# One level of Strassen's algorithm in the first MLP product of a two-layer hybrid backbone

## The chip, the core and the metric

The kernel runs on one core of one Trainium2 chip. The metric is the device time of one execution in microseconds. Five engines work beside each other, each in its own fixed order of instructions: PE multiplies matrices (PEld loads its weights), DVE is the vector engine, ACT the scalar engine, POOL the general one, SP issues transfers; POOL and ACT can issue them too.

## What is computed

Two layers over 512 latent tokens of 1024 features, and in the first layer 256 context tokens as well. Each layer has a mixer (recurrence, attention, pooling, one output projection) and an MLP, both behind a modulated norm and both added with a gate:

```python
def _mlp(h, w1, w2):
    return jnp.square(jax.nn.relu(h @ w1)) @ w2
...
        x = x + g1 * y_lat
        x = x + g2 * _mlp(_modulate(_rmsnorm(x, g_norm2[l]), sh2, sc2), w_ff1[l], w_ff2[l])
        if not last:
            h = h + cg1 * y_ctx
            h = h + cg2 * _mlp(_modulate(_rmsnorm(h, g_norm2[l]), csh2, csc2), w_ff1[l], w_ff2[l])
```

`w1` is 1024 x 4096, `w2` 4096 x 1024, all in fp32.

## The kernel before

All activations stand with features on the 128 partitions and tokens along the row. A product is done in three passes of float32r matmuls: every operand is split into a high part (an ACT cast) and a low part (what the cast left over, a DVE subtraction), and `mm3` (L241) adds high x high, high x low and low x high. Weights come in blocks of 128x1024 (512 KB), streamed in the order of use by `Weights` (loads three blocks ahead, four buffers `raw`; the split into `whi`, L142, and `wlo`, L143, two blocks ahead, ten buffers).

The end of the mixer takes the eight tiles of the output projection one after the other: PE's products `wo` go into one of two large accumulators (`psA`), DVE adds the gated result to the residual tile (`add_to`, L1189), ACT and DVE make the modulated tile's parts `xh` and `xl` (`scaled`, L467 and L468), and `square` adds the tile's squares to the running sum on POOL (`acc`, L456). The shift of the modulation is carried as two further columns, so that 770 columns stream in layer 0 and 514 in layer 1. The norm's 1/rms is not needed until the products come out: `nsum` (L478) and `spread` (L498) put it on all partitions as `rb`.

`ffn` works by chunks of 128 hidden features. For one chunk `gemm_mod` streams eight tiles x three passes x two column segments, 48 matmuls. `ff1_out` scales by `rb` (`tf`, L539), adds the bias and clips (ACT, L544, L546), squares, and keeps the high and low parts `hh` and `hl` in SBUF (L1255 to L1257). Eight chunks of the first product alternate with eight tiles of the second (`ff2`, 24 matmuls of a segment each), which adds its gated result to the resident residual tile (L1276). In layer 0's MLP, "fills" run on DVE between the chunks: 56 items of modulation for later (`mod_rows`, `junk`, L413), each of two passes over 128x1024.

The order on each engine comes from a scheduler in the building framework that follows the order of the code and the buffers' release; the mixer's steps are listed by hand in `ORDER`. SBUF holds 47 row buffers of 776 columns in two classes: 18 "flow" tiles whose names are in `FLOW`, and 29 others.

## Time and profile before

| | |
|---|---|
| three runs | 1651.52, 1651.87, 1656.19 us; median 1651.87 |
| profiled execution | span 1650.7 us (its only time), 24064 instructions |
| PE | 1582.8 us busy, 96% |
| PE weight load | 1380.6 us, 84% |
| DVE | 1122.0 us, 68% |
| ACT | 680.4 us, 41% |
| POOL | 368.2 us, 22% |
| mean granted PE clock | 0.978 of full speed |
| memory traffic | 184.57 MB, 112 GB/s |

The profile records one execution. Its page gives each engine's busy time, groups of like instructions with the idle time before them and what ended it, and the transfers. The trace behind it can be asked for timelines, windows and single tiles. A busy time counts instructions that overlap once.

The layers follow each other: layer 0's mixer until 443 us, its MLP until 985, layer 1's mixer until 1283, its MLP until the end.

### The profile page before, as it was taken

The numbers are of one execution on the slowest core, as the hardware profiler recorded it, in microseconds if no ns is written. First come the engines' busy times: TensorE is split into PE (matmuls) and PEld (weight loads), VectorE is DVE, ScalarE is ACT, GpSimd is POOL, SyncE is SP. The second block draws the span as 40 slices with busy tenths as digits, with TensorE's granted clock in tenths as the row PEclk, the third lists the DMA queues.
The fourth block names the chain that finished last, engine by engine and source line by source line (L and its number), as shares of the span: only waits on it lengthen the run. The fifth ranks groups of instructions, "written<-read, shape, count | busy, mean of one in ns | idle before, by whom it ended". The sixth has DMA issues, their size and how long they took to land.

```text
span 1650.7 us, 24064 instructions
## 1 busy us (share of the span) xinstructions
PE 1582.8 (96%) x9519; PEld 1380.6 (84%) x9519; DVE 1122.0 (68%) x1810; ACT 680.4 (41%) x1078; POOL 368.2 (22%) x376
## 2 busy tenths in 40 slices
PE   5989999999999999999999999888999999999998
PEld 3668888889888888888888889787888989989897
DVE  8797888998767557837737646698987654545352
ACT  5557556646433123123213333745665432323131
POOL 4175434542300000000000232356454000000000
PEclk7999989999999999999999999999999999999999
DMA  6545211354234423524523430320334323323302
GB/s 251 198 150 185 81 58 37 94 185 152 82 97 144 142 89 119 187 78 128 166 90 120 142 109 21 121 71 20 97 122 141 103 90 96 97 90 93 100 27 102
DMA packets 54016, 184.57 MB, mean 112 GB/s; under 512 B 6624, under 2 KB 7264, under 8 KB 53904
## 3 DMA queue, kind: packets, MB, share of 16 engines
q1 hardware_dynamic: 49680, 166.49, 31.0%
q0 software_dynamic: 4224, 16.55, 2.8%
...
## 4 chain that ended last, share of the span: by engine, by line
PE 76%; DVE 15%; issue 4%; ACT 3%; POOL 1%; DMA 1%; SPq 0%; DVEq 0%; ACTq 0%; POOLq 0%
PE f L241 55%; PE wo L241 5%; PE inps L241 4%; PE sc L241 3%; DVE wlo L143 3%; PE tp L914 2%; DVE p L897 1%; PE modps L369 1%; DVE junk L413 1%; PE qp L241 1%; PE pv L936 1%; PE pv L937 1%; DVE ptl L922 1%; PE gps L241 1%; PE kns L823 1%
## 5 line engine op out<-in xcount | busy, mean ns | idle before, releaser
L142 ACT CAST whi<-raw 128x1024 fp32r<-128x1024 f32 x210 | 219.6, 1048 | 657.2 <-PE f L241 550.7
L143 DVE TENSOR_TENSOR wlo<-raw,whi 128x1024 fp32r<-128x1024 f32 x210 | 276.3, 1318 | 35.3 <-ACT whi L142 32.6
L241 PE MATMUL f<-xh,whi 128*128 128x258 f32 (+2 forms) x1024 | 234.6, 310 | 1.0 <-DVE tf L539 1.0
L241 PE MATMUL f<-xl,whi 128*128 128x258 f32 (+2 forms) x1024 | 234.5, 310 | 0.0
L241 PE MATMUL f<-xh,wlo 128*128 128x258 f32 (+2 forms) x1024 | 234.1, 310 | 0.0
L241 PE MATMUL f<-hh,wlo 128*128 128x512 f32 (+1 forms) x768 | 232.2, 356 | 0.0
L241 PE MATMUL f<-hl,whi 128*128 128x512 f32 (+1 forms) x768 | 231.9, 356 | 0.0
L241 PE MATMUL f<-hh,whi 128*128 128x512 f32 (+1 forms) x768 | 231.3, 356 | 0.0
L1276 DVE SCALAR_TENSOR_TENSOR xo<-f,mod,xo 128x512 f32<-128x512 f32 x96 | 60.5, 658 | 195.6 <-PE f L241 195.6
L413 DVE SCALAR_TENSOR_TENSOR junk<-modraw,cb 128x1024 bf16<-128x1024 f32 x128 | 161.8, 1275 | 21.9 <-DMA modraw<-in_wb_dram 21.5
L241 PEld LDWEIGHTS f<-xh,whi 128*128 128x128 f32 x1024 | 157.8, 189 | 12.5 <-PE f L241 1.2
L241 PEld LDWEIGHTS f<-xl,whi 128*128 128x128 f32 x1024 | 158.2, 189 | 11.4
L241 PEld LDWEIGHTS f<-xh,wlo 128*128 128x128 f32 x1024 | 157.9, 189 | 11.3
L539 DVE TENSOR_TENSOR tf<-f,rb 128x770 f32<-128x770 f32 (+1 forms) x64 | 52.8, 826 | 159.1 <-PE f L241 150.2
L241 PEld LDWEIGHTS f<-hh,whi 128*128 128x128 f32 x768 | 126.5, 188 | 22.4
L241 PEld LDWEIGHTS f<-hh,wlo 128*128 128x128 f32 x768 | 126.3, 188 | 22.5
L241 PEld LDWEIGHTS f<-hl,whi 128*128 128x128 f32 x768 | 126.4, 188 | 22.3
L463 POOL CAST xh<-mod 128x2 fp32r<-128x2 f32 x24 | 10.6, 441 | 466.8 <-PE f L241 466.8
L225 POOL TENSOR_SCALAR p<-p,sm 128x768 f32<-128x768 f32 (+1 forms) x80 | 70.4, 880 | 117.3 <-DVE sm L899 81.1
L241 PE MATMUL inps<-xh,whi 128*128 128x512 f32 (+1 forms) x352 | 87.3, 331 | 7.3 <-ACT xh L467 5.6
L305 ACT ACTIVATE p<-p,sm 128x768 f32<-128x768 f32 (+1 forms) x80 | 68.2, 853 | 57.4 <-DVE p L897 56.8
L241 PE MATMUL inps<-xl,whi 128*128 128x512 f32 (+1 forms) x352 | 86.4, 326 | 3.1 <-DVE xl L468 3.1
...
## 6 DMA issues: line engine op xcount, KB each, us to landing
...
kb<-kd POOLq DMA_DIRECT2D x16, 384.0 KB, 4.3
x<-in_x_dram SPq DMA_DIRECT2D x8, 384.0 KB, 7.0
xo<-in_x_dram SPq DMA_DIRECT2D x8, 384.0 KB, 3.4
xp<-xo POOLq DMA_DIRECT2D x8, 384.0 KB, 3.5
xo<-xp SPq DMA_DIRECT2D x8, 384.0 KB, 3.1
xd<-xo POOLq DMA_DIRECT2D x8, 256.0 KB, 2.4
```

Source lines behind the costliest of these rows:

```text
L142: nc.scalar.copy(hi, raw)
L143: nc.vector.tensor_tensor(lo, raw, hi.bitcast(F32), ALU.subtract)
L225: return self.nc.gpsimd.tensor_scalar(out, in_, scale, 0.0, ALU.mult, ALU.add)
L241: nc.tensor.matmul(ps, lhsT=a[:, ca], rhs=b[:, cb], start=first and i == 0, stop=last and i == 2)
L305: ins = self.nc.scalar.activation(out, in_, func, **kw)
L369: nc.tensor.matmul(ps[0:4, :], lhsT=self.ct[:, kk * 2 + j, :], rhs=w[:, j * 512:(j + 1) * 512], start=(kk == 0 and j == 0 and i == 0), sto ...
L413: nc.vector.scalar_tensor_tensor(junk, r, 1.0, c, ALU.mult, ALU.mult, accum_out=acc[l, g][:, v * 16 + i:v * 16 + i + 1])
L539: nc.vector.tensor_tensor(t[:, 0:n], ps[:, o:o + n], self.rb[:, 0:n], ALU.mult)
L823: nc.tensor.matmul(ps[:, tt:tt + 7:6], lhsT=sq[:, tt * 128:(tt + 1) * 128], rhs=self.cst[:, CST_SELK:CST_SELK + 2], start=True, stop=True)
L897: nc.vector.tensor_scalar(p[:, 0:keys], s, rq[:, qt:qt + 1], None, ALU.mult, ALU.min, accum_out=nb)
L914: nc.tensor.transpose(ps[:, j * 256 + q * 128:j * 256 + (q + 1) * 128], ps2[q][:, kt * 128:(kt + 1) * 128], self.ident)
L1276: nc.vector.scalar_tensor_tensor(x[:, a:a + e], ps[:, a:a + e], mod[:, v, 8 + m:9 + m], x[:, a:a + e], ALU.mult, ALU.add)
```

## The change

The 1024 x 4096 product is cut into 2 x 2 x 2 blocks: features in two halves of four tiles (`KORD` pairs tile j with j + 4), hidden features in two halves (chunk u with u + 16), tokens in two halves of 384 (layer 0) or 256 columns, each with two shift columns, 386 or 258. One level of Strassen's algorithm in Winograd's form makes seven products of them. A "unit" is a pair of chunks: seven products of four tiles x three passes, 84 matmuls; 16 units a layer. Products 1, 2, 6, 5 and 7 run in the unit, 3 and 4 after the first product of the next one.

For the stream, `stream_ops` makes per pair of tiles four differences on POOL and seven split operands `xq` (ACT cast, DVE subtraction), kept for the whole first product. For the weights, `weight_ops` makes per unit three differences on DVE (`ws`: t7, t6, t3); the sum of two blocks is made by a DMA that POOL issues and that adds one half of a loaded block to a half of the other, in SBUF. Seven split operands `wo` of 128x512 follow. From the accumulators, ACT copies three products out, DVE adds three and scales by `rb`.

All of the first product runs before all of the second. The hidden values go to memory unsplit (`hd`, issued by ACT) and the residual tiles too (`xf`, issued by POOL); the second product loads its hidden tiles again, one per tile of output, and splits them. Of the fills, 20 run in the first product and 36 in the second; those of layer 1 that nobody reads for the context are left out (`streams`).

The core of the diff:

```diff
-    "a2 acc gate hh hl inv knsq latn lsq mix p ps2 pth ptl pvt qlh qll rb t th u yh ylru z",
-    "a2 gate hh hl latn lsq lxp mxl p ps2 pth ptl pvt qlh qll row sq t th u yl ylru z",
+    "a2 acc gate inv knsq latn lsq mix p ps2 pth ptl pvt qlh qll rb t th u yh ylru z xz ya yb rr hz xr tt",
+    "a2 gate latn lsq lxp mxl p ps2 pth ptl pvt qlh qll row sq t th u yl ylru z xz ya yb rr hz xr tt",
 )
 NSLOT, NFLOW = 29, 18
-NGF = D_FF // 128 // GF
+NCH = D_FF // 128
+UNITS = NCH // 2
+GF = 8
+NGROUP = NCH // GF
+GROUPS = tuple(tuple(u + h * UNITS for u in range(g * GF // 2, (g + 1) * GF // 2) for h in range(2)) for g in range(NGROUP))
+KORD = tuple(j + h * KD // 2 for j in range(KD // 2) for h in range(2))
+FIRST, LATER = (1, 2, 6, 5, 7), (3, 4)
...
-        while self.split < min(len(self.order), at + 1 + self.splits):
+        while self.split < min(self.loaded, at + 1 + self.splits):
             name = self.order[self.split]
+            if name[1] == "ff1":
+                self.split += 1
+                continue
...
+    def get_raw(self, name):
...
+        self.loads = 1 if self.order[min(self.at + 4, len(self.order) - 1)][1] == "ff1" else 3
+        self.advance(self.at)
+        self.at += 1
+        return self.raw.pop(name)
...
+        def add_to(h, i, src):
+            acc, _ = pss.pop((h, i))
+            m = KORD[i]
             x = self.slot("xo")
...
-        s, sh = self.norm_scale(l, 2)
-        self.X, self.xs2 = [None] * KD, [None] * KD
-        for m in range(KD):
-            if m == 0:
+        ff = self.ff = FeedForward(self, l)
+        for i in range(KD):
+            if i == 0:
                 for j in [j for h, j in pss]:
                     project(1, j, LATE[-1:])
-            elif (1, m) not in pss:
-                project(1, m, LATE)
-            self.X[m] = add_to(1, m, self.xp[l])
-            self.xs2[m] = self.scaled(m, self.X[m], s, sh, ctx)
-            self.square(m, self.X[m], n)
...
+            elif (1, i) not in pss:
+                project(1, i, LATE)
+            ff.stream(i, add_to(1, i, self.xp[l]))
...
+class FeedForward:
+    def __init__(self, K, l):
+        self.K, self.nc, self.l = K, K.nc, l
...
+        self.n = T if self.ctx else L
+        self.nh = self.n // 2
+        self.n1 = self.nh + 2
+        self.s, self.sh = K.norm_scale(l, 2)
+        self.xq = [None] * (KD // 2)
...
+        self.jobs = [Hidden(self, u) for u in range(UNITS)]
+    def parts(self, hi, lo, src):
+        self.nc.scalar.copy(hi, src)
+        self.nc.vector.tensor_tensor(lo, src, hi.bitcast(F32), ALU.subtract)
+    def stream_ops(self, blocks, n, q):
+        nc, sub = self.nc, ALU.subtract
+        b11, b12, b21, b22 = blocks
+        def part(p, src):
+            q[p] = self.K.slot("xq", F32R)
+            self.parts(q[p][:, 0:n], q[p][:, n:2 * n], src)
...
+        part(1, b11)
+        part(2, b21)
+        nc.gpsimd.tensor_tensor(t[5], b12, b11, sub)
+        nc.gpsimd.tensor_tensor(t[6], b22, t[5], sub)
+        part(6, t[6])
+        part(5, t[5])
+        nc.gpsimd.tensor_tensor(t[7], b22, b12, sub)
+        nc.gpsimd.tensor_tensor(t[4], b21, t[6], sub)
+        part(7, t[7])
+        part(3, b22)
+        part(4, t[4])
+    def weight_ops(self, names, w):
+        nc, K = self.nc, self.K
+        a, t = [], {}
+        def part(p, src):
+            w[p] = K.wp.tile([128, 1024], F32R, tag="w", name="wo")
+            self.parts(w[p][:, 0:512], w[p][:, 512:1024], src)
+        def begin():
...
+            nc.vector.tensor_tensor(t[7], a[0], a[2], ALU.subtract)
+            nc.gpsimd.dma_start(out=a[2], in_=a[3], accum_op=ALU.add)
+            part(1, a[0])
+        def second():
+            nc.vector.tensor_tensor(t[6], a[2], a[0], ALU.subtract)
+            part(6, t[6])
+        def third():
+            nc.vector.tensor_tensor(t[3], a[1], t[6], ALU.subtract)
+            part(7, t[7])
+        return [begin, lambda: part(2, a[1]), second, lambda: part(5, a[2]), third, lambda: part(3, t[3]),
+                lambda: part(4, a[3])]
+    def product(self, ps, p, w, n, start):
+        for k in range(KD // 2):
+            wh, wl = (w[p][:, h * 512 + k * 128:h * 512 + (k + 1) * 128] for h in range(2))
+            xh, xl = self.xq[k][p][:, 0:n], self.xq[k][p][:, n:2 * n]
+            for j, (a, b) in enumerate(((wh, xh), (wh, xl), (wl, xh))):
+                self.nc.tensor.matmul(ps, lhsT=a, rhs=b, start=start and k == 0 and j == 0,
+                                      stop=k == KD // 2 - 1 and j == 2, skip_group_check=True)
+    def stream(self, i, x):
+        K, nc = self.K, self.nc
+        m = KORD[i]
...
+        nc.gpsimd.dma_start(out=K.xf[self.l, m, :, 0:self.n], in_=x[:, 0:self.n])
+        z = self.z[m] = K.slot("xz")
+        for c, e, v, t in self.pieces(2):
+            nc.scalar.activation(z[:, c:c + e], x[:, t:t + e], AF.Copy, scale=self.s[:, v, m:m + 1])
+        gap = z[:, 0:2 * self.n1].rearrange("p (h c) -> p h c", h=2)[:, :, self.nh:self.n1]
+        sh = self.sh[:, :, m].unsqueeze(1) if self.ctx else self.sh[:, 0, m:m + 1].unsqueeze(1)
+        nc.gpsimd.tensor_copy(gap, sh.to_broadcast([128, 2, 2]))
+        K.square(m, x, self.n)
+        if i % 2:
+            j = i // 2
+            n1 = self.n1
+            z1, z2 = self.z.pop(j), self.z.pop(j + KD // 2)
+            q = self.xq[j] = {}
+            self.stream_ops((z1[:, 0:n1], z1[:, n1:2 * n1], z2[:, 0:n1], z2[:, n1:2 * n1]), n1, q)
...
+    def load_hidden(self, c):
+        K, n = self.K, self.n
+        z = K.slot("hz")
+        K.load(z[:, 0:n], K.hd[self.l, c, :, 0:n])
+        hi, lo = K.slot("hh", F32R), K.slot("hl", F32R)
+        self.parts(hi[:, 0:n], lo[:, 0:n], z[:, 0:n])
+        self.h[c] = hi, lo
...
+    def run(self):
...
+        prev = None
+        for i, job in enumerate(self.jobs + [None]):
+            nxt = list(self.jobs[i + 1].prep) if i + 1 < len(self.jobs) else (
+                [lambda c=c: self.load_hidden(c) for c in GROUPS[0]] if job else [])
+            seq = [(job, p) for p in FIRST] if job else []
+            late = [(prev, p) for p in LATER] if prev else []
+            seq = seq[:1] + late + seq[1:]
+            for at, (jb, p) in enumerate(seq):
+                jb.do(p)
...
+                upto = -(-len(nxt) // (len(seq) - at))
+                for step in nxt[:upto]:
+                    step()
+                del nxt[:upto]
+            if job:
+                fill(early * (i + 1) // UNITS)
+            prev = job
+        self.x = {}
+        for m in KORD:
+            self.x[m] = K.slot("xr")
+            K.load(self.x[m][:, 0:self.n], K.xf[self.l, m, :, 0:self.n])
...
+class Hidden:
+    def __init__(self, ff, u):
+        self.ff, self.u, self.w = ff, u, {}
+        self.prep = ff.weight_ops([(ff.l, "ff1", c) for c in (u, u + UNITS)], self.w)
+    def do(self, p):
+        ff, K, nc = self.ff, self.ff.K, self.ff.nc
+        n = ff.n1
+        if p == 1:
+            self.bank = K.psA("f1")
+            self.ya, self.yb = K.slot("ya"), K.slot("yb")
+        b1, b3 = self.bank[:, 0:n], self.bank[:, 512:512 + n]
+        if p == 2:
+            self.other = K.psB("f1")
+        ps = {2: self.other[:, 0:n] if p == 2 else None, 5: b3, 3: b3}.get(p, b1)
+        ff.product(ps, p, self.w, n, p in (1, 2, 5))
+        half = slice(0, n), slice(n, 2 * n)
+        if p == 1:
+            nc.scalar.copy(self.ya[:, half[0]], ps)
+        elif p == 6:
+            nc.scalar.copy(self.ya[:, half[1]], ps)
+        elif p == 5:
+            nc.scalar.copy(self.yb[:, half[1]], ps)
+        elif p == 2:
+            nc.vector.tensor_tensor(self.ya[:, half[0]], ps, self.ya[:, half[0]], ALU.add)
+        elif p == 7:
+            nc.vector.tensor_tensor(self.yb[:, half[1]], ps, self.yb[:, half[1]], ALU.add)
+        elif p == 3:
+            nc.vector.tensor_tensor(self.ya[:, half[1]], ps, self.ya[:, half[1]], ALU.add)
+            nc.vector.tensor_tensor(self.ya[:, 0:2 * n], self.ya[:, 0:2 * n], ff.rb[:, 0:2 * n], ALU.mult)
+            self.out(self.u, self.ya)
+        else:
+            nc.vector.tensor_tensor(self.yb[:, half[0]], ps, ff.rb[:, half[0]], ALU.mult)
+            nc.vector.tensor_tensor(self.yb[:, half[1]], self.yb[:, half[1]], ff.rb[:, half[1]], ALU.mult)
+            self.out(self.u + UNITS, self.yb)
+    def out(self, c, y):
+        ff, K, nc = self.ff, self.ff.K, self.ff.nc
+        r = K.slot("rr")
+        for at, e, v, t in ff.pieces(2):
+            nc.scalar.activation(r[:, t:t + e], y[:, at:at + e], AF.Relu, bias=y[:, ff.nh + v:ff.nh + v + 1])
+        nc.scalar.activation(r[:, 0:ff.n], r[:, 0:ff.n], AF.Square)
+        nc.scalar.dma_start(out=K.hd[ff.l, c, :, 0:ff.n], in_=r[:, 0:ff.n])
...
-    rawp = ctx.enter_context(tc.tile_pool(name="raw", bufs=4))
+    rawp = ctx.enter_context(tc.tile_pool(name="raw", bufs=5))
     wp = ctx.enter_context(tc.tile_pool(name="wts", bufs=10))
...
-    nc = _bacc.Bacc("TRN2", target_bir_lowering=False, num_devices=1)
+    nc = _bacc.Bacc("TRN2", target_bir_lowering=False, num_devices=1, dynamic_dma_scratch_size=4096)
```

The order in which DVE's instructions stand at the end of layer 0's mixer, before, about the tiles in the middle (`xo<-wo` is the gated add, `xl` a low part, `wlo` that of weights):

```order
L1189 SCALAR_TENSOR_TENSOR xo<-wo,mod_1_975,xo 128x512
L1189 SCALAR_TENSOR_TENSOR xo<-wo,mod_1_975,xo 128x256
L468 SCALAR_TENSOR_TENSOR xl<-xo,s_2_4563,xh 128x512
L468 SCALAR_TENSOR_TENSOR xl<-xo,s_2_4563,xh 128x256
L143 TENSOR_TENSOR wlo<-raw,whi 128x1024
L1189 SCALAR_TENSOR_TENSOR xo<-wo,mod_1_975,xo 128x512
```

The same place on DVE after the change, from behind the adds of the second pair of tiles to the first add of the third (`ws` are the weight differences, `wo<-ws` and `wo<-raw` low parts of weights, `xq` those of the stream, `tt` POOL's differences):

```order
L1348 TENSOR_TENSOR ws<-raw 128x512
L1302 TENSOR_TENSOR xq<-xz,xq 128x386 x2
L1353 TENSOR_TENSOR ws<-raw 128x512
L1357 TENSOR_TENSOR ws<-raw,ws 128x512
L1302 TENSOR_TENSOR wo<-ws,wo 128x512
L1302 TENSOR_TENSOR wo<-raw,wo 128x512
L1302 TENSOR_TENSOR xq<-tt,xq 128x386 x2
L1302 TENSOR_TENSOR wo<-ws,wo 128x512 x2
L1302 TENSOR_TENSOR xq<-tt,xq 128x386
L1302 TENSOR_TENSOR xq<-xz,xq 128x386
L1302 TENSOR_TENSOR xq<-tt,xq 128x386
L1219 SCALAR_TENSOR_TENSOR xo<-wo,mod_1_977,xo 128x512
```

The add of a tile stood one tile's low parts behind the add before it; now it stands behind seven low parts of the pair before, and here behind eight operations of weights too, the second difference (L1353) among them, which reads what the accumulating DMA writes.

On PE, what follows the last output tile of layer 0, before:

```order
L241 MATMUL wo<-yh,wlo 128x256
L241 MATMUL f_4874<-xh,whi 128x512
L241 MATMUL f_4874<-xh,whi 128x258
L241 MATMUL f_4874<-xl,whi 128x512
L241 MATMUL f_4874<-xl,whi 128x258
```

and after the change (`f_5011` is the second product of unit 0, `f_4981` its first, sixth and later ones, `f_5121` the first of unit 1):

```order
L268 MATMUL wo<-yh,wlo 128x256
L1369 MATMUL f_5011<-xq,wo 128x386 x3
L1369 MATMUL f_4981<-xq,wo 128x386 x9
L1369 MATMUL f_5121<-xq,wo 128x386 x9
L1369 MATMUL f_4981<-xq,wo 128x386
L1369 MATMUL f_5121<-xq,wo 128x386
L507 MATMUL nsum<-ones,acc 128x1 x6
L1369 MATMUL f_5011<-xq,wo 128x386
L1369 MATMUL f_4981<-xq,wo 128x386 x2
L1369 MATMUL f_5121<-xq,wo 128x386 x2
L1369 MATMUL f_5011<-xq,wo 128x386 x2
L1369 MATMUL f_4981<-xq,wo 128x386 x24
```

Twice three matmuls of `f_5011` stand further ahead, between output tiles. Those of the last pair of tiles begin with the single `f_4981`.

In the middle of layer 1's first product a chunk took these four rows of DVE before:

```order
L539 TENSOR_TENSOR tf<-f_12762,rb 128x514
L143 TENSOR_TENSOR wlo<-raw,whi 128x1024
L1256 TENSOR_TENSOR r<-r 128x512
L1257 TENSOR_TENSOR hl<-r,hh 128x512
```

From the first weight difference of a unit to the second and third, after the change:

```order
L1348 TENSOR_TENSOR ws<-raw 128x512
L1523 TENSOR_TENSOR ya<-ya,rb 128x516
L1302 TENSOR_TENSOR wo<-ws,wo 128x512
L1302 TENSOR_TENSOR wo<-raw,wo 128x512
L1526 TENSOR_TENSOR yb<-f_13353,rb 128x258
L1302 TENSOR_TENSOR wo<-raw,wo 128x512
L1353 TENSOR_TENSOR ws<-raw 128x512
L1357 TENSOR_TENSOR ws<-raw,ws 128x512
```

Five operations lie between the first difference (t7, with whose operands' release the accumulating DMA is issued) and the second (t6, which waits for it).

## Rows read from the trace of the kernel before

**Rows 1.** The page's first part: busy time, share, instructions of each engine.

```profile
PE 1582.8 (96%) x9519; PEld 1380.6 (84%) x9519; DVE 1122.0 (68%) x1810; ACT 680.4 (41%) x1078; POOL 368.2 (22%) x376
```

**Rows 2.** Windows: length, then busy time of each engine, granted PE clock, DMA.

```profile
416.70:443.30 26.60, 26.06 (x149) 22.56 (x148) 22.84 (x31) 15.74 (x24) 14.52 (x16) 1.00 0.23 81
...
985.00:1240.00 255.00, 234.83 (x1524) 209.10 (x1523) 210.76 (x394) 140.77 (x259) 117.56 (x108) 0.98 0.23 76
...
1309.00:1470.00 161.00, 161.00 (x1000) 144.51 (x1000) 75.81 (x86) 48.00 (x57) 0.00 (x0) 1.00 0.29 93
```

**Rows 3.** The page's costliest groups: busy, mean ns, idle before, releaser.

```profile
L241 PE MATMUL f<-xh,whi 128*128 128x258 f32 (+2 forms) x1024 | 234.6, 310 | 1.0 <-DVE tf L539 1.0
```

**Rows 4.** Timeline of PE in the first product, layer 0, then layer 1.

```profile
478.63 0.51 PE L241 MATMUL f<-xh,wlo 128*128 128x512 f32 x2
478.99 0.51 PE L241 MATMUL f<-xh,whi 128*128 128x512 f32 x2
...
1300.16 0.40 PE L241 MATMUL f<-xh,whi 128*128 128x256 f32 x2
1300.40 0.40 PE L241 MATMUL f<-xl,whi 128*128 128x256 f32 x2
```

**Rows 5.** The tile tf, three chunks of layer 0 and of layer 1.

```profile
L539 DVE TENSOR_TENSOR tf<-f,rb x3: 959/960/960, 470.7 to 487.6; 128x770 f32<-128x770 f32 x3
...
L539 DVE TENSOR_TENSOR tf<-f,rb x3: 693/693/693, 1308.9 to 1320.3; 128x514 f32<-128x514 f32 x3
```

**Rows 6.** Groups of DVE, each shape apart: busy, mean ns, idle before.

```profile
L413 DVE SCALAR_TENSOR_TENSOR junk<-modraw,cb 128x1024 bf16<-128x1024 f32 x128 | 161.8, 1275 | 21.9 <-DMA modraw<-in_wb_dram 21.5
...
L1257 DVE TENSOR_TENSOR hl<-r,hh 128x512 fp32r<-128x512 f32 x32 | 22.2, 692 | 1.1
```

**Rows 7.** Timeline of DVE in layer 1's first product.

```profile
1299.83 0.69 DVE L1257 TENSOR_TENSOR hl<-r,hh 128x512 fp32r<-128x512 f32 x1
1300.44 0.68 DVE L1256 TENSOR_TENSOR r<-r 128x512 f32<-128x512 f32 x1
```

**Rows 8.** Groups of POOL, each shape apart: an issue of a transfer.

```profile
L1310 POOL DMA_DIRECT2D xd<-xo x8 | 4.6, 571 | 46.9 <-DVE xo L1276 46.9
```

**Rows 9.** The page's DMA issues: count, KB each, median us to landing.

```profile
kb<-kd POOLq DMA_DIRECT2D x16, 384.0 KB, 4.3
x<-in_x_dram SPq DMA_DIRECT2D x8, 384.0 KB, 7.0
...
xd<-xo POOLq DMA_DIRECT2D x8, 256.0 KB, 2.4
```

**Rows 10.** Timelines of DVE and PE where the mixers end.

```profile
416.68 2.19 DVE L1189 SCALAR_TENSOR_TENSOR xo<-wo,mod,xo 128x512 f32<-128x512 f32 x4 [2.98 <-PE wo L241]
...
442.82 0.51 PE L241 MATMUL wo<-yh,wlo 128*128 128x512 f32 x2
443.17 0.52 PE L241 MATMUL f<-xh,whi 128*128 128x512 f32 x2
...
1283.26 0.40 PE L241 MATMUL f<-xh,whi 128*128 128x256 f32 x2
```

**Rows 11.** Timelines of DVE and POOL at the end of layer 0's mixer.

```profile
426.75 1.14 DVE L1189 SCALAR_TENSOR_TENSOR xo<-wo,mod,xo 128x512 f32<-128x512 f32 x2
...
426.87 1.87 POOL L456 TENSOR_TENSOR acc<-acc,sq 128x768 f32<-128x768 f32 x1 [2.32 <-ACT sq L447]
...
429.70 1.85 POOL L456 TENSOR_TENSOR acc<-acc,sq 128x768 f32<-128x768 f32 x1
430.36 2.27 DVE L143 TENSOR_TENSOR wlo<-raw,whi 128x1024 fp32r<-128x1024 f32 x1 [0.67 <-ACT whi L142]
...
440.24 1.22 DVE L143 TENSOR_TENSOR wlo<-raw,whi 128x1024 fp32r<-128x1024 f32 x1
```

**Rows 12.** The tile acc: durations in ns, min/median/max, first and last start, shapes.

```profile
L456 POOL TENSOR_TENSOR acc<-acc,sq x24: 1291/1855/2730, 17.3 to 1284.0; 128x768 f32<-128x768 f32 x18, 128x512 f32<-128x512 f32 x6
```

**Rows 13.** Timeline of PE at the start of the program.

```profile
7.61 0.63 PE L369 MATMUL modps<-whi,ct 128*4 128x512 f32 x1
8.04 0.63 PE L369 MATMUL modps<-wlo,ct 128*4 128x512 f32 x1
```

221 lines of the change are left out of this document (114 added, 107 removed).

## The prediction, written before the change was run

> **What bounds the kernel now.** The page's first part comes first: PE is busy for 96% of the span, the vector engine for 68%, POOL for 22% [rows 1]. The windows tell whether that holds in the stages that change: at the end of layer 0's mixer PE works 26.06 of 26.60 us, in the MLP of layer 1 all 161.00 of 161.00 at a granted clock of 1.00 (2.4 GHz), while DVE needs 75.81 [rows 2]. The groups say that PE's first MLP product waited 1.0 us in the whole run [rows 3]. So the MLP is bound by the columns that stream through PE; everything else has cover, and a saved matmul is a saved matmul only as long as that stays so.
>
> PE's timeline gives the price of a column. A pair of 512+258 columns starts every 0.353 us in layer 0, a pair of 256+258 every 0.2375 in layer 1 [rows 4]. 256 columns more cost 0.1155 us, 0.45 ns each; so a matmul of 258 columns takes about 0.119 us and one of 386 about 0.119 + 128 x 0.45 = 0.176 us. Finished chunks of the first product follow each other every 8.45 us in layer 0 (three starts over 16.9 us) and every 5.7 us in layer 1 [rows 5]: 270.4 and 182.4 us for 32 chunks.
>
> **What the change saves on PE.** Seven products of half size replace eight: 16 units x 84 = 1344 matmuls per layer, against 1536 pieces. Layer 0: 1344 x 0.176 = 236.5, a gain of **33.9 us**. Layer 1: 1344 x 0.119 = 159.9, a gain of **22.5 us**. Together 56.4. The Trainium skill (TensorE: Matmul & The Clock Gate, Back-to-back issue gap) gives N/2.4 GHz + 2.5 ns for one isolated matmul. By it both forms would be cheaper than these rows have them, and the gain some 51 us; the rows are of this kernel's own weight-load and matmul stream, so they stand.
>
> **What it costs in the steady part.** The cover shrinks. A unit of layer 1 lasts 84 x 0.119 = 10.0 us on PE. DVE gets ten operations on 128x512 (three differences of weights, seven low parts), three adds from the accumulators on 258 columns, and four widths of 258 in the scaling. A 512 operation takes 692 ns by itself [rows 6], but the next independent one starts 0.61 us after it [rows 7]. With 0.61 for 512 and 0.35 for 258 (the same 0.45 us per 256 less) the sum is 6.1 + 1.05 + 1.3 = 8.5, some 8.8 with dependent pairs; by full durations 9.7. So DVE has 0.3 to 1.2 us to spare where it had half the time. In layer 0 a unit lasts 14.8; the 386-wide work makes it 9.6, and 1.25 modulation items at 2 x 1.15 add 2.9 (1275 ns by duration [rows 6]): 12.5, spare 2.3. I count nothing for these, since PE still ends last; ACT has about 8.4 of 10.0 and 9.8 of 14.8 by the same count.
>
> The weight difference t6 waits for the accumulating transfer. It is behind t7 on DVE with one scaling and four low-part or scaling operations between, 2.9 us in layer 1, and 1.1 spare makes 4.0. Behind the waiting t6 stand t3, the sixth and third low parts and the adds that give PE its accumulators back. No row shows an accumulating transfer or one inside SBUF. The nearest: issuing on POOL takes 0.57 [rows 8]; on its queue 256 KB from SBUF to memory land after 2.4 us and 384 KB from memory after 4.3, and on another queue at the program's start, where all loads come at once, 384 KB took 7.0 [rows 9]. I take 3.6, nearer the upper of POOL's two since an accumulation reads two operands: 3.6 + 0.57 = 4.2 us. That overruns 4.0 by 0.2, 16 times: **+3 us** in layer 1 (with only 0.3 of DVE's reserve it would be 16; with 2.4 us nothing; with 7.0 us 57), nothing in layer 0, where cover and reserve come to 5. The Trainium skill (DMA: Bandwidth & Descriptors, Anatomy of one DMA — SWDGE (gpsimd) path) has about 2 us plus bytes at 436 GB/s, here 2.6: by it this term is 0. No run here shows it.
>
> The hidden values now go to memory and back (25 MB in layer 0, 17 in layer 1, 10 more for the residual stream). Each is used tens of us after it was written, and a load is issued a tile ahead, 8.45 or 5.5 us against the 3.5 or so of a transfer of its size; so I count nothing. The second product gets one hidden tile to split per tile (0.88 us on DVE) beside its weights: at most 6.6 of 8.45 us in layer 0, 2.6 of 5.5 in layer 1, hidden behind PE. Where the two products meet, the first eight hidden tiles need slots that the last unit still holds: 0 to 4 us a layer, taken as **+1** in all. The 32 modulation passes saved lie under PE: 0.
>
> **What it costs at the mixer's end.** This is the large price. Before, each output tile needs on DVE only its gated add and a low part, and PE goes from output projection to first product with no gap: the last output pair starts at 442.82, the first of the new product at 443.17, in layer 1 at 1283.26 [rows 10]. Now a pair of tiles goes through ACT's scaling, four POOL differences (a chain: t5, t6, t4), seven ACT casts and seven low parts. In DVE's order the gated adds of the next pair stand behind this, for the third pair also behind t6 of the first weights, and PE's output tiles wait for those adds (two accumulators). POOL and DVE don't overlap there: a weights' low part that takes 1.22 us alone took 2.27 beside a 1.85 us sum of POOL, starting at 430.36 and ending 1.1 after that sum [rows 11]. So their work adds up. POOL's sums take 1.855 us at the median, most of them on 768 columns, and 1.29 at the least, on 512 [rows 12]; so 386 take about 1.02, 258 about 0.74.
>
> Layer 0, from 418.9 when the first two adds are done (2.19 us from 416.68 [rows 10]): first pair four differences 4.1, a sum 1.9, seven low parts 3.9, two weight parts 1.3, start 1.2 = 12.4; second 4.1 + 3.7 + 3.9 + eight weight operations 5.2 = 16.9; third 4.1 + 3.7 + 3.9 and 2.8 of chain and adds = 14.5; last 4.1 + 1.9 + 3.9 and 2.1 = 12. PE runs on without gaps from 418.9 + 55.8 = 474.7, with some 48 matmuls (8.4 us) done before. Start moved from 443.3 to 466.3: **+23.0 us**. Layer 1 from 1266: 8.7 + 15.2 + 10.0 + 8.7 = 42.6, so 1308.6 less 48 x 0.119 = 1302.9 against 1283.3, less the 1.0 us wait of [rows 3]: **+18.6 us**. In these gaps PE's clock may fall: at the start of the program 512 columns take 0.43 us each, 1.2 GHz [rows 13]. Two us lost at each layer's restart: **+4**; 0 and 8 are the ends, since in the mixer, where PE is idle for 8%, the granted clock is 0.98 [rows 2].
>
> **Sum:** -33.9 - 22.5 + 3 + 1 + 23.0 + 18.6 + 4 = -6.8 us against the span of 1650.7. The median of the runs is 1.2 above that span, so 1651.9 - 6.8 = **1645 us**. A measurement of this kernel can tell about 0.3%, 5 us, from no change.
>
> **Rivals.** *The gaps at the mixer's end are half as long.* If only single operations exclude each other, POOL's row alone decides: 16 differences, seven sums, nine issues and the small copies are 38 us in layer 0 and about 30 in layer 1. PE then runs on from 457 and 1296: 18 and 12 us earlier, with no clock lost for long: 1645 - 30 = **1615**. For it: the gated adds, which read the accumulators, weren't held (1.14 us at 426.75 beside a sum from 426.87 on [rows 11]), and casts on ACT overlap with both. Against: the low parts, which are most of DVE's new work, were held, and DVE's order chains the pairs.
>
> *Slower: the accumulating transfer is the bound.* Place: t6 in every unit, in DVE's strict order. At a landing 5 us after issue, 5.6 in all, the overrun is 1.6 in layer 1 and 0.6 in layer 0 (16 units each, 26 + 10 less the 3 counted): 1645 + 33 = **1678**. It decides from 0.4 us of overrun a unit beyond mine (a landing at about 4.0). For it: 4.3 of the same queue, and an accumulation must read two operands; DVE, at 85 to 97%, can't catch up. Against: 2.4 for the same size.
>
> *They cancel.* Pairs 10% longer, or the clock at 8, give about 1652, no change; this is the upper part of my forecast's own range, 1636 to 1657.
>
> **How the numbers follow.** Forecast 0.40 (half of it over 5 us faster), short gaps 0.27, slow transfer or DVE-bound 0.33. Faster by over 0.3%: 0.27 + 0.20 = 0.47; within: 0.18; slower: 0.02 + 0.33 = 0.35. The range takes in most of both rivals: 1614 to 1684; the likeliest case alone 1636 to 1657.
>
> **What would show it.** PE's rows must count 2688 matmuls of the new product, 0.176 and 0.119 us apart where dense; if layer 1's units are 10.0 us apart with PE at 100%, the steady part costs nothing. A wait of t6 on the transfer, over 1 us each time, would prove the second rival. In the windows PE should idle for some 15 to 25 us between 420 and 475 and as much around 1270 to 1309, ended by the low parts of the new stream parts; if those gaps are under 10 us, the first rival holds. The second product should keep its spacing of 8.45 and 5.5 us; if not, the trip to memory isn't hidden, which none of my terms holds.

## The result and the profile after

The changed kernel takes 1703.87 us (median, 1701.99 to 1705.57) where the kernel before takes 1652.94 on the same chip: a ratio of **1.0313 [1.0298, 1.0328]**, 51 us slower, where 1645 was forecast. The profiled execution has a span of 1700.2 us, 49.5 more than before. Of the runs below, e1, e6 and v0 each had one execution at a much lower clock, which their medians include and their ratios leave out.

The first part of the page of the kernel after (busy time, share, instructions):

```profile
PE 1562.3 (92%) x9135; PEld 1376.4 (81%) x9135; DVE 1233.1 (73%) x2098; ACT 845.2 (50%) x1536; POOL 422.1 (25%) x440
```

Against [rows 1], PE has 384 matmuls fewer, as the change promises, but its busy time is only 20.5 us less where the forecast takes 56.4 off: the matmuls that are left take longer on average. Its idle time (span less busy) has grown by more than that, from 67.9 us to 137.9. The windows say in which stages. Of the kernel after (stretch, length, busy time of PE, PEld, DVE, ACT, POOL with counts, granted clock, DMA share, GB/s):

```profile
416.00:480.00 64.00, 48.41 (x230) 41.97 (x229) 49.07 (x63) 33.81 (x73) 34.38 (x41) 0.84 0.34 117
...
500.00:700.00 200.00, 184.78 (x1007) 178.34 (x1005) 150.90 (x254) 109.67 (x216) 10.43 (x12) 0.99 0.52 166
...
800.00:900.00 100.00, 100.00 (x574) 87.53 (x573) 68.08 (x102) 25.23 (x28) 0.00 (x0) 1.00 0.70 239
...
1283.20:1340.00 56.80, 40.50 (x183) 33.07 (x181) 42.31 (x64) 29.48 (x73) 31.41 (x45) 0.82 0.35 116
...
1345.00:1510.00 165.00, 154.34 (x1220) 148.38 (x1218) 129.17 (x230) 112.39 (x231) 11.22 (x13) 1.00 0.57 165
```

The first and fourth rows are the mixers' ends: PE idles 15.6 and 16.3 us there, as foretold, where the end of layer 0's mixer was nearly full before [rows 2]. The third row is the second product of layer 0, with PE full: the trip of the hidden values to memory is hidden. The second and fifth rows are the surprise: the units of the first product in their steady run. One matmul starts every 200/1007 = 0.1986 us in layer 0 and every 165/1220 = 0.1352 in layer 1, not every 0.176 and 0.119. The waits name the releasers. Of the kernel after (engine, tile and line that wait, tile and line waited for: total us, count, longest):

```profile
PE f L1369 <- DVE yb L1526: 21.2, 27, 2.0
...
PE wo L268 <- DVE xo L1219: 19.4, 7, 6.6
...
DVE ws L1353 <- DMA raw<-raw: 36.8, 28, 3.7
```

The second line is the mixers' ends (output tiles that wait for the gated adds). The first and third are new waits in the units. PE's timeline shows the first of them at least once per unit; layer 0, then layer 1 of the kernel after (start, us, engine, line, instruction, count, idle before and its releaser):

```profile
567.44 15.20 PE L1369 MATMUL f<-xq,wo 128*128 128x386 f32 x84 [0.47 <-DVE yb L1526]
583.93 10.37 PE L1369 MATMUL f<-xq,wo 128*128 128x386 f32 x57 [1.30 <-DVE yb L1526]
...
1421.79 10.71 PE L1369 MATMUL f<-xq,wo 128*128 128x258 f32 x84 [0.52 <-DVE yb L1526]
1433.02 10.71 PE L1369 MATMUL f<-xq,wo 128*128 128x258 f32 x84 [0.52 <-DVE yb L1526]
```

A unit of 84 matmuls takes 16.49 us here in layer 0 and 11.2 in layer 1. Line 1526 is the scaling that empties the accumulator of product 4, the last of a unit. PE stops for it because in its order product 1 of the unit after next, which uses the same buffer, stands right behind product 4: the accumulator's round trip (last matmul, DVE's scaling, semaphore, first matmul) lies open once a unit. The other wait, on DVE, in layer 1 of the kernel after, with POOL's issue of the accumulating transfer between t7 and the t6 that needs it:

```profile
1429.99 0.68 DVE L1348 TENSOR_TENSOR ws<-raw 128x512 f32<-128x512 f32 x1
1431.20 0.86 POOL L1349 DMA_DIRECT2D raw<-raw  x1 [10.36 <-DVE ws L1348]
1434.73 0.69 DVE L1353 TENSOR_TENSOR ws<-raw 128x512 f32<-128x512 f32 x1 [0.85 <-DMA raw<-raw]
```

The transfer's row among the DMA issues on the page (KB each, median us to landing):

```profile
raw<-raw POOLq DMA_DIRECT2D x32, 256.0 KB, 3.6
```

The page counts these 3.6 us from the start of the issue: from 1431.20 to the start of t6 at 1434.73 are 3.53. So the 0.86 us of the issue on POOL (0.57 for a plain transfer [rows 8]) are in them. t6 waits 0.85 us in the unit shown, 1.3 in the mean (36.8/28).

### The profile page after: what moved, and what is told of

It reads as the page before. It is cut to its first block, busy times and chain, and to the rows that moved or that the text cites. A ratio compares the mean times of both kernels' runs of the same rounds, so it can differ in the third digit from the quotient of the medians.

```text
span 1700.2 us, 24547 instructions
## 1 busy us (share of the span) xinstructions
PE 1562.3 (92%) x9135; PEld 1376.4 (81%) x9135; DVE 1233.1 (73%) x2098; ACT 845.2 (50%) x1536; POOL 422.1 (25%) x440
## 4 chain that ended last, share of the span: by engine, by line
PE 49%; DVE 13%; ACT 6%; issue 5%; DMA 4%; POOL 2%; ACTq 0%; POOLq 0%; DVEq 0%
PE f L268 26%; PE f L1369 13%; PE wo L268 3%; DMA raw<-raw 3%; PE inps L268 2%; ACT rr L1534 2%; PE sc L268 2%; DVE wo L1302 1%; ACT wo L1301 1%; DVE xq L1302 1%; PE tp L943 1%; DVE wlo L159 1%; DVE p L926 1%; DVE junk L441 1%; ACT rr L1535 1%
## 5 line engine op out<-in xcount | busy, mean ns | idle before, releaser
L1369 PE MATMUL f<-xq,wo 128*128 128x386 f32 (+1 forms) x2688 | 427.7, 318 | 42.2 <-DVE yb L1526 21.2
L1369 PEld LDWEIGHTS f<-xq,wo 128*128 128x128 f32 x2688 | 408.7, 193 | 59.5 <-DVE yb L1526 28.3
L158 ACT CAST whi<-raw 128x1024 fp32r<-128x1024 f32 x146 | 152.1, 1047 | 320.8 <-PE f L268 136.7
L159 DVE TENSOR_TENSOR wlo<-raw,whi 128x1024 fp32r<-128x1024 f32 x146 | 199.5, 1372 | 35.3 <-ACT whi L158 16.5
L1433 DVE SCALAR_TENSOR_TENSOR xr<-f,mod,xr 128x512 f32<-128x512 f32 x96 | 60.5, 658 | 172.0 <-PE f L268 172.0
L1301 ACT CAST wo<-raw 128x512 fp32r<-128x512 f32 x128 | 78.6, 617 | 59.5 <-PE f L1369 59.1
L1302 DVE TENSOR_TENSOR wo<-raw,wo 128x512 fp32r<-128x512 f32 x128 | 91.2, 716 | 22.0 <-ACT wo L1301 21.2
L1301 ACT CAST wo<-ws 128x512 fp32r<-128x512 f32 x96 | 58.4, 619 | 88.6 <-PE f L1369 46.3
L268 PE MATMUL inps<-xh,wlo 128*128 128x512 f32 (+1 forms) x352 | 86.5, 327 | 0.0
L951 DVE TENSOR_TENSOR ptl<-tp,pth 128x512 fp32r<-128x512 f32 (+1 forms) x136 | 71.8, 557 | 7.4 <-ACT pth L243 6.8
```

Source lines behind the costliest of these rows:

```text
L158: nc.scalar.copy(hi, raw)
L159: nc.vector.tensor_tensor(lo, raw, hi.bitcast(F32), ALU.subtract)
L268: nc.tensor.matmul(ps, lhsT=a[:, ca], rhs=b[:, cb], start=first and i == 0, stop=last and i == 2)
L951: nc.vector.tensor_tensor(lo[:, c], ps[:, a * 256:b * 256], hi[:, c].bitcast(F32), ALU.subtract)
L1301: self.nc.scalar.copy(hi, src)
L1302: self.nc.vector.tensor_tensor(lo, src, hi.bitcast(F32), ALU.subtract)
```

## The experiments

Three causes are to be told apart: the **accumulators** (PE's order, and the tile of two halves that products 1, 6, 7, 4 and 5, 3 share: `b1` and `b3` of line 1505), the **accumulating transfer**, and the **stop at the mixer's end** with its operations on POOL. All ratios are to the kernel before.

### e1: PE in the order of the code

```diff
+                ins = self.nc.tensor.matmul(...)
+                if pin and k == 0 and j == 0 and self.K.w.order is not None:
+                    self.K.tc.keep_in_program_order(ins)
```

> The edit pins each of the seven products of a unit on PE behind the product that the code names before it, so that the first product of a unit no longer stands right behind the fourth of the unit two before. Theory A (round trip): in the changed kernel PE waits at each unit until DVE has scaled the fourth product out of the accumulator (0.5 us idle in layer 1, 0.5 to 1.3 in layer 0, and as much again in slow first matmuls); the unit lasts 16.5 us in layer 0 and 11.2 in layer 1 against 15.0 and 10.0 dense. Without it both units come close to dense: 15 x 1.3 + 15 x 1.1 = some 36 us less, about 1668 us, and the wait of PE for the scaled product yb is gone from the list of waits. Theory B (the accumulating DMA holds DVE and so sets the unit): under 8 us less, above 1695, the unit stays near 11.2 in layer 1 and PE waits for low parts of weights instead.

Measured: 1787.79 us, 1.0794 [1.0744, 1.0845], far worse. In PE's timeline of e1 one unit now has three stops (its lines 1516, 1518 and 1524 are the copies of products 6 and 5 and the add of product 3):

```profile
601.11 2.41 PE L1369 MATMUL f<-xq,wo 128*128 128x386 f32 x12 [1.09 <-ACT ya L1516]
604.61 6.65 PE L1369 MATMUL f<-xq,wo 128*128 128x386 f32 x36 [1.09 <-ACT yb L1518]
612.13 6.67 PE L1369 MATMUL f<-xq,wo 128*128 128x386 f32 x36 [0.87 <-DVE ya L1524]
```

The first row is product 5, 12 matmuls that start a sum in the second half of the tile. It waits for the copy of product 6 out of the first half, with which it shares no value: the two halves are waited for as one tile. The other two stops are of the same kind: product 7, in the first half, waits for the copy of product 5 out of the second, and product 4 for the add of product 3. I take the order of the changed kernel, with fewer stops, for the scheduler's way round that; no run shows why it chose it. The fixed order alone is no remedy; the shared tile had to be tried.

### e2: the accumulating transfer left out

```diff
-            nc.gpsimd.dma_start(out=a[2], in_=a[3], accum_op=ALU.add)
-            nc.vector.tensor_tensor(t[6], a[2], a[0], ALU.subtract)
+            nc.vector.tensor_tensor(t[6], a[3], a[0], ALU.subtract)
```

> The accumulating DMA is left out and the second weight difference reads the block that was to be added, so that one weight sum is missing from the product; all other work is as in the changed kernel. Theory A (round trip of the accumulator): the order on PE keeps the first product right behind the fourth, so the unit stays near 16.3 and 11.2 us and the time is within 8 us of 1704. Theory B (the DMA's wait sets the unit): the unit falls to 15 and 10 us, 1670. In either case DVE's 37 us of waiting for the DMA are gone.

Measured: 1695.08 us, 1.0260 [1.0233, 1.0288]: 9 us of the 51. PE's timeline of e2 in layer 1 (its line 1525 is 1526 of the kernel after):

```profile
1414.00 10.43 PE L1368 MATMUL f<-xq,wo 128*128 128x258 f32 x84 [0.97 <-DVE yb L1525]
1425.40 10.43 PE L1368 MATMUL f<-xq,wo 128*128 128x258 f32 x84 [0.97 <-DVE yb L1525]
```

A unit lasts 11.4 us with no transfer at all. So as long as the accumulators' round trip is there, the transfer is not what sets the unit in layer 1.

### e3: the four stream differences on DVE

```diff
-        nc.gpsimd.tensor_tensor(t[5], b12, b11, sub)
+        nc.vector.tensor_tensor(t[5], b12, b11, sub)
...
```

> The four differences of each pair of stream tiles are made on DVE instead of POOL. Theory C (exclusion): at the mixer's end the low parts of DVE waited as long as POOL ran sums and differences back to back (5.2, 4.2 and 3.4 us for a 0.5 us operation); with the differences on DVE at about 0.5 us each a pair loses POOL's 4 x 0.9 us and gains 4 x 0.5, and the chain over two engines goes; 2 to 4 us less per pair, four pairs, two layers, with less time at half clock: 20 us less, about 1684. Theory D (the order alone, the adds behind the pair's low parts, makes the gap): the pair stays about as long, within 6 us of 1704.

Measured: 1690.72 us, 1.0221 [1.0201, 1.0241], 15 us better than the change, where exclusion was to bring 20. The window of e3 at the end of layer 0's mixer: PE's granted clock is 0.92 there, where the change has 0.84, and PE does 271 matmuls, not 230:

```profile
416.00:480.00 64.00, 52.84 (x271) 46.39 (x270) 57.84 (x98) 40.80 (x86) 22.70 (x26) 0.92 0.40 131
```

DVE and POOL hold each other there. Timelines of the kernel after, POOL and then DVE:

```profile
439.81 2.24 POOL L485 TENSOR_TENSOR acc<-acc,sq 128x768 f32<-128x768 f32 x1
441.61 1.26 POOL L1321 TENSOR_TENSOR tt<-xz,tt 128x386 f32<-128x386 f32 x1
442.44 1.41 POOL L1324 TENSOR_TENSOR tt<-xz 128x386 f32<-128x386 f32 x1
443.41 1.25 POOL L1325 TENSOR_TENSOR tt<-xz,tt 128x386 f32<-128x386 f32 x1
...
439.86 5.23 DVE L1302 TENSOR_TENSOR xq<-xz,xq 128x386 fp32r<-128x386 f32 x1 [0.87 <-ACT xq L1301]
```

One low part, issued 0.05 us after POOL's sum, ends 0.43 us after the last of four POOL operations. The Trainium skill (SBUF — State Buffer, Who interferes with whom) says that a DVE instruction with two SBUF inputs contends with a GpSimd instruction that reads SBUF; these rows agree, with the 5.23 us. The low parts of this shape as a group (busy us, mean ns, idle before), in the kernel after and in e3:

```profile
L1302 DVE TENSOR_TENSOR xq<-xz,xq 128x386 fp32r<-128x386 f32 x12 | 20.8, 1739 | 8.3 <-ACT xq L1301 8.3
...
L1302 DVE TENSOR_TENSOR xq<-xz,xq 128x386 fp32r<-128x386 f32 x12 | 6.3, 548 | 0.0
```

### e5: the gated adds two tiles ahead of the stream parts

```diff
-            ff.stream(i, add_to(1, i, self.xp[l]))
+            xs[i] = add_to(1, i, self.xp[l])
+            if i >= 2:
+                ff.stream(i - 2, xs.pop(i - 2))
+        for i in (KD - 2, KD - 1):
+            ff.stream(i, xs.pop(i))
```

> The gated add of an output tile is written two tiles ahead of the stream work, so that adds and PE's output tiles no longer stand behind the low parts of the pair before. Theory D (order): PE's waits of output tiles for the adds (10.6 us in layer 0, 8.4 in layer 1) go and output tiles end some 15 us earlier in each layer, but the stream's parts themselves remain; if the parts are the longer chain (theory C), the idle time only moves behind the output tiles and the time falls by less than 8 us (1696 or more). If the order is the cause, 20 us less, about 1684.

Measured: 1699.16 us, 1.0274 [1.0253, 1.0295], 6 us better. Two lines of e5's waits:

```profile
PE wo L268 <- DVE xo L1219: 9.0, 5, 4.9
...
PE f L1374 <- DVE yb L1531: 21.0, 27, 2.6
```

The output tiles' wait halves (19.4 to 9.0), but the stream parts then come later, and the units' stop is untouched.

### e6: products 5 and 3 get a tile of their own

```diff
-        b1, b3 = self.bank[:, 0:n], self.bank[:, 512:512 + n]
+        if p == 5:
+            self.third = K.psB("f1")
+        b1, b3 = self.bank[:, 0:n], self.third[:, 0:n] if p in (3, 5) else None
```

> Products 5 and 3 get an accumulator tile of their own (one bank) instead of the second half of the tile that products 1, 6, 7 and 4 use. Theory E (the tile is waited for as a whole): PE's waits for ACT and DVE in the first product come from the shared tile, and the order on PE, with the first product of a unit behind the fourth of an earlier one, is what the scheduler made to get around them; with two tiles the scheduler orders anew and PE's idle time within the units (some 20 us in all, and the slow first matmuls behind each wait) mostly goes: 1675 to 1685. Rival A (the round trip at the fourth product is real, by data): PE still waits once a unit, within 6 us of 1704.

Measured: 1676.59 us, 1.0130 [1.0102, 1.0158], 30 us better (0.0183 x 1653). PE's timeline of e6 in layer 0 has 670 matmuls, nearly eight units, without a stop, where in the kernel after every unit has one; then comes one long stop, near the end of the product. The row of DVE shows what stands behind it, a t6 that waits for the transfer:

```profile
569.02 119.08 PE L1369 MATMUL f<-xq,wo 128*128 128x386 f32 x670 [0.49 <-DVE yb L1528]
695.41 17.27 PE L1369 MATMUL f<-xq,wo 128*128 128x386 f32 x84 [7.31 <-ACT ya L1516]
...
687.01 0.69 DVE L1353 TENSOR_TENSOR ws<-raw 128x512 f32<-128x512 f32 x1 [4.36 <-DMA raw<-raw]
```

The scaling of the unit stands behind this t6 on DVE; ACT waits 9.21 us for that scaling, and the copy that PE waits for stands behind it on ACT.

Windows and waits of e6:

```profile
500.00:700.00 200.00, 190.99 (x1059) 189.05 (x1058) 158.15 (x269) 115.45 (x229) 10.44 (x12) 0.98 0.60 182
...
1330.00:1470.00 140.00, 132.73 (x1079) 130.36 (x1078) 112.07 (x206) 96.25 (x208) 11.22 (x13) 1.00 0.58 168
...
DVE ws L1353 <- DMA raw<-raw: 57.3, 28, 4.4
```

1059 matmuls where there were 1007, and the wait for the transfer has grown from 36.8 to 57.3 us, its median landing on the page from 3.6 to 4.6: with the round trip gone, the transfer is the next thing to end late. In layer 0 that shows almost only in the one long stop.

### e7: e1 and e6 together

> Own tiles for products 5 and 3, and the products pinned in the order of the code, as in the run that was slower than the changed kernel (1788 us, with three waits of about 1.1 us a unit). Theory E: two of these three waits were for copies out of the other half of the same tile and vanish; 1670 to 1685, 100 us below the pinned order with the shared tile. Rival A: the waits are for data, the time stays near 1780.

Measured: 1683.46 us, 1.0181 [1.0162, 1.0200]. With the shared tile the fixed order cost 80 us over the change (1.0794 against 1.0313); with separate tiles it costs 8 over e6. So what hurt in e1 was the tile; the order by itself brings nothing. Of e1's three stops mostly one is left, before product 7, and what it waits for is now the copy of product 6 out of the buffer that it writes:

```profile
PE f L1369 <- ACT ya L1518: 20.9, 19, 2.3
```

### e8: e6 and e3 together

> Own tiles for products 5 and 3, and the stream's differences on DVE. If the two losses are separate (accumulators in the steady part, exclusion of POOL and DVE at the mixer's end), their gains add: 13 us from the differences and some 25 from the tiles, 1665. If they share a cause (DVE's load), the sum falls short of that by 10 us or more, 1677 and above.

Measured: 1660.28 us, 1.0047 [1.0028, 1.0066], 14 us better than e6: as much as e3 alone brought (15): the two gains add.

### e9: e8 with the order of e1 and the adds of e5

> Own tiles, pinned order, differences on DVE and the gated adds two tiles ahead. If transition and accumulators are the two losses, most of them is recovered: 1645 to 1660, level with the kernel before (about 1653). If the steady part has another bound (DVE, or the accumulating DMA), it stays above 1670 and PE waits in the units for low parts of weights.

Measured: 1673.7 us, 1.0124 [1.0105, 1.0142], 13 us worse than e8. Adding up the remedies fails here. It stays above 1670, but not by waits for low parts of weights: PE waits for the copy of product 6 (L1523 in e9), as in e7, so the fixed order brings its own stop back:

```profile
PE f L1374 <- ACT ya L1523: 21.8, 18, 2.6
```

### v0 and v1: the sums of squares on DVE too; then the adds ahead

Edits: that of e8, and the running sum of squares of the stream tiles on DVE; v1 has e5's adds beside it.

```diff
-            add = nc.vector if k == KD - 1 else self.at("sq.a")
+            add = nc.vector if vec or k == KD - 1 else self.at("sq.a")
...
-        K.square(m, x, self.n)
+        K.square(m, x, self.n, vec=True)
```

> Own tiles, the stream's differences on DVE, and now the sums of squares at the mixer's end on DVE too, so that POOL computes nothing that reads two rows there. Theory C (exclusion): what is left of DVE's long operations in that place (3.2 and 2.2 us for a difference of 0.55, beside POOL's sums, in the run with own tiles and differences on DVE) goes; DVE pays 0.95 for each sum instead of up to 1.85 of waiting: 4 to 8 us less than that run's 1660, 1653 to 1657. Theory D (the order of the adds): no gain, 1658 or more.

> As the run with sums on DVE, and the gated adds written two tiles ahead. With POOL out of the way the waits of output tiles for adds (6.2 + 2.6 us in layer 0, 5.4 + 2.8 in layer 1 of the run with own tiles and differences on DVE) are due to the order alone; they go, and with them some of the time at half clock: 8 to 14 us below the run with sums on DVE, 1642 to 1648, which would be just faster than the kernel before. If DVE's own work at the mixer's end is the bound, the idle time moves to the new product's first matmuls and the gain is under 4 us.

Measured: v0 1665.59 us, 1.0062 [1.0037, 1.0087], no better than e8; v1 1677.75, 1.0146 [1.0129, 1.0164], worse, where both expectations for it had a gain. The wait for the transfer in v1 is the largest of all runs, and the median landing on its page the longest:

```profile
DVE ws L1358 <- DMA raw<-raw: 75.2, 29, 5.3
...
raw<-raw POOLq DMA_DIRECT2D x32, 256.0 KB, 5.2
```

The loss lies in layer 1's units: the same window in v0, then in v1:

```profile
1340.00:1460.00 120.00, 113.45 (x918) 112.17 (x917) 96.23 (x178) 82.13 (x176) 9.49 (x11) 0.99 0.59 171
...
1340.00:1460.00 120.00, 105.72 (x836) 102.83 (x835) 85.17 (x158) 72.36 (x159) 8.65 (x10) 0.99 0.54 154
```

### v2: v1 with the weight sum on DVE

```diff
-            nc.gpsimd.dma_start(out=a[2], in_=a[3], accum_op=ALU.add)
+            nc.vector.tensor_tensor(a[2], a[2], a[3], ALU.add)
```

> As the run with adds ahead, and the one weight sum is made by DVE (0.61 us a unit) instead of the accumulating DMA. If the DMA's wait still costs DVE more than that (28 waits, 54 us in all, in the run with own tiles and differences on DVE), and DVE's waits reach PE, 3 to 8 us less; if PE's cover hides the wait, the same within 3 us; if DVE is the bound in layer 1 (its unit goes from about 8.8 to 9.4 of 10.0 us), 3 to 10 us more.

Measured: **1630.92 us, 0.9872 [0.9854, 0.9891]**, faster than both kernels. v1 and v2 differ in this one line, and by 45 us, where the largest gain expected was 8. Windows of v2:

```profile
416.00:470.00 54.00, 47.81 (x251) 42.08 (x250) 49.51 (x91) 36.32 (x79) 15.81 (x17) 0.94 0.34 121
...
500.00:700.00 200.00, 199.35 (x1122) 197.91 (x1121) 173.04 (x288) 124.67 (x242) 0.00 (x0) 1.00 0.54 186
...
1310.00:1450.00 140.00, 139.87 (x1159) 139.39 (x1158) 125.42 (x229) 105.39 (x223) 0.00 (x0) 1.00 0.52 170
```

PE is full in the units while DVE is busy for 125.42 of 140, 90%; the mixer's end still has gaps.

### w1 to w4: which of the edits does it

All four have the weight sum on DVE, as the diff of v2 shows. w1 is the changed kernel with that line alone; w2 has e6's tile besides; w3 has v0's edits besides (without the adds ahead); w4 is v2 with the shared tile put back.

> The changed kernel with one edit: the weight sum on DVE instead of the accumulating DMA; shared accumulator tile, differences and sums on POOL as in the change. If the shared tile's waits set the unit as long as they are there (theory E), DVE's earlier t6 buys little: the run that left the sum out gained 9 us, so 1693 to 1700. If the accumulating DMA is the larger loss by itself, 1680 or less.

> Own accumulator tiles and the weight sum on DVE, the mixer's end as in the change. Against own tiles alone (1677): if the DMA's wait cost what it did in the pair of runs with all of the mixer's end on DVE (47 us), 1630 to 1640; if that pair was a special case of its order, and only the idle time that the trace of own tiles shows in the units (10 us a layer) goes, 1655 to 1662.

> Own tiles, differences, sums of squares and the weight sum on DVE, but the gated adds not written ahead. Against the fastest kernel so far (1631): if the adds ahead are worth the waits of output tiles that the run without them showed (9.7 us in layer 0, 7.9 in layer 1) and the clock, 1640 to 1648; if they only move the idle time, 1628 to 1636.

> The fastest kernel so far with the accumulators put back into one shared tile. If the shared tile costs by itself, as theory E has it (27 us in the changed kernel), 1650 to 1660; if it cost only in company with the DMA's wait, 1630 to 1638.

| kernel | tile | weight sum | median us | ratio to before |
|---|---|---|---|---|
| the change | shared | transfer | 1703.87 | 1.0313 [1.0298, 1.0328] |
| w1 | shared | DVE | 1692.04 | 1.0236 [1.0212, 1.0259] |
| e6 | own | transfer | 1676.59 | 1.0130 [1.0102, 1.0158] |
| w2 | own | DVE | 1655.32 | 1.0011 [0.9994, 1.0027] |
| w3: w2, differences and sums on DVE | own | DVE | 1642.01 | 0.9928 [0.9907, 0.9948] |
| v2: w3, adds ahead | own | DVE | 1630.92 | 0.9872 [0.9854, 0.9891] |
| w4: v2 | shared | DVE | 1668.90 | 1.0098 [1.0079, 1.0118] |
| v1: v2 | own | transfer | 1677.75 | 1.0146 [1.0129, 1.0164] |

The first four rows are the whole table of two edits: the transfer alone is worth 13 us, the tile alone 30, both 50. That is 7 more than the two by themselves, and about as much as these four intervals leave open (7 us). The 45 us between v1 and v2 and the 20 between e6 and w2 do differ: what the transfer costs depends on the order around it. In w4 the tile costs 37 us, more than the 27 expected. Windows of layer 0's and layer 1's units, in w1 and then in w2:

```profile
500.00:700.00 200.00, 191.09 (x1051) 184.36 (x1051) 165.43 (x278) 114.19 (x221) 0.00 (x0) 1.00 0.47 158
...
1345.00:1485.00 140.00, 127.10 (x1006) 122.29 (x1005) 113.37 (x202) 93.63 (x190) 0.00 (x0) 1.00 0.44 139
```

```profile
500.00:700.00 200.00, 199.37 (x1125) 198.81 (x1124) 171.38 (x289) 122.11 (x242) 0.00 (x0) 1.00 0.52 176
...
1330.00:1470.00 140.00, 140.00 (x1165) 140.00 (x1164) 127.31 (x232) 105.48 (x223) 0.00 (x0) 1.00 0.51 166
```

In w2's windows PE hardly stops (199.37 of 200 us, 140 of 140). Its rows give the price of a dense matmul: 200/1125 = 0.1778 us and 140/1165 = 0.1202.

## Why the prediction was wrong

The forecast was -6.8 us, the span shows +49.5. With w2's dense spacing the ledger of the change is:

| term of the sum | predicted us | measured us | from |
|---|---|---|---|
| seven products, dense: 1344 x 0.1778 and 1344 x 0.1202, against 270.4 and 182.4 | -56.4 | -52.3 | w2's windows |
| units less than dense, layer 0: 1344 x (0.1986 - 0.1778) | 0 | +28.0 | windows after |
| the same, layer 1: 1344 x (0.1352 - 0.1202) | +3 | +20.2 | windows after |
| mixers' ends, clock and where the products meet | +46.6 | +53.6 | what is left |
| sum | -6.8 | +49.5 | |

**The step that failed** is the one on the steady part: "I count nothing for these, since PE still ends last". It compared DVE's sum of durations in a unit with PE's, and that sum was right: w2 and v2 run dense with DVE busy at 86 to 91%. What it left out is latency. A unit has four accumulations that are emptied and written again, and the text priced the emptying as work of DVE, never as a round trip that PE waits for. The order of PE's instructions could have shown it: product 1 of the unit after next stands right behind product 4, on the same buffer. e6, e7 and w4 show the cause in the tile of two halves: own tiles take 30 us off the change, and putting the shared tile back into v2 costs 37. w1, which has the shared tile and no transfer, still loses 1344 x (200/1051 - 0.1778) = 16.8 us in the units of layer 0 and 1344 x (140/1006 - 0.1202) = 25.5 in layer 1; w2, with own tiles, loses nothing there.

**The accumulating transfer** was priced at +3, in layer 1 alone. Its sum, 3.6 + 0.57, counts the issue twice, since the page's times start with the issue. By luck the total is right: in the unit shown it is 4.06 us from the end of t7 (1430.67) to t6, because POOL's issue begins 0.53 us after t7. What failed is the cover. DVE reached t6 after 3.2 us, not 4.0: the 1.1 us that DVE has to spare lay elsewhere in the unit.

"Nothing in layer 0, where cover and reserve come to 5" failed for the change, and layer 1 came out the other way. Without the transfer (w1) layer 0's units gain 1344 x (0.1986 - 200/1051) = 11 us, and layer 1's lose 5 (140/1006 = 0.1392 a matmul, where the change has 0.1352). With own tiles (e6 against w2) the transfer costs in both: e6's window of layer 0 loses 200 - 1059 x 0.1778 = 11.7 us, 7.3 of it in the one stop before 695.41, that of layer 1 140 - 1079 x 0.1202 = 10.3. These 22 us are near the 20 between the two kernels. The rival of the slow transfer named the right place, t6, and gave 1678; the landing that it asked for, 5.6 us in all, is not what the change has (3.6), and it missed the second cause that stands beside it. The rival of the short gaps is refuted by the gaps of 15.6 and 16.3 us.

**Terms that held.** 2688 matmuls of the new product, 0.178 and 0.120 us apart where dense (0.176 and 0.119 predicted). The second product keeps its pace: a tile of 48 matmuls takes 48 x 100/574 = 8.4 us in layer 0, where 8.45 was taken. PE idle for 15 to 25 us at each mixer's end: 15.6 and 16.3. The chain of pairs in layer 0 was to end at 431, 448, 463 and 475; the low parts of the four pairs ended at 433, 451, 465 and 480, and the first two adds were done 3.5 us late (422.4 against 418.9). That DVE's and POOL's work adds up there is borne out by the row of 5.23 us and by e3 and w3 (15 and 14 us less when POOL's part goes to DVE). The terms of that end together came out 7 us too small; they are what is left in the ledger, not measured by themselves. w2, where the steady loss is gone, agrees with this sum: -52.3 + 53.6 = +1.3, and its ratio of 1.0011 is +1.8 us.

**The clock** was taken at 2 us lost a layer. In the windows it is 0.84 and 0.82 over 64 and 57 us, where before the mixer's end had 1.00 [rows 2]: PE drops to the lower level again and again, not once. The windows of three such stretches of layer 0, and PE's timeline in the second, of the kernel after:

```profile
435.00:439.00 4.00, 4.00 (x16) 3.43 (x16) 1.59 (x3) 3.10 (x7) 3.76 (x4) 0.57 0.24 98
...
449.00:456.00 7.00, 3.61 (x11) 3.10 (x12) 4.39 (x9) 5.05 (x12) 2.70 (x4) 0.52 0.14 56
...
466.00:473.00 7.00, 6.04 (x19) 6.04 (x20) 4.77 (x8) 4.89 (x10) 5.57 (x8) 0.51 0.54 203
```

```profile
452.39 1.01 PE L268 MATMUL wo<-yh,whi 128*128 128x512 f32 x2 [6.63 <-DVE xo L1219]
453.20 0.84 PE L268 MATMUL wo<-yl,whi 128*128 128x512 f32 x2
...
456.12 0.51 PE L268 MATMUL wo<-yh,whi 128*128 128x512 f32 x2
456.47 0.55 PE L268 MATMUL wo<-yl,whi 128*128 128x512 f32 x2
```

After 6.63 us without work, pairs start 0.64 to 0.8 us apart at the lower level (1.2 GHz), and from 456 on 0.35 apart. PE works 13.7 us in these three stretches at about half speed, which loses some 7 us; a fourth in layer 0 (476 to 480) and three in layer 1 (from 1299, 1313 and 1326, 13.6 us of work) bring it to about 15 us for both layers, where 4 was taken and 8 was the upper end. That is an estimate of PE's loss from these rows and an upper bound for the span, since PE waits for adds between these stretches anyway. It could cover the 7 missing; no run separates the clock from the waits.

**Left open.** Why the first adds come 3.5 us late, and the second layer's mixer takes some 2 us longer. Why the adds ahead cost 14 us with the transfer (v0 to v1) and bring 9 without (w3 to v2): the loss is in layer 1's units, where v1 has the longer landings, but no run shows what makes them longer. In v2 the mixers' ends, the clock and what else is left still cost about 35 us (its span is 17.6 below the one before, of 52.3 saved).
